# The second MLP matrix in seven products on six input tiles instead of four

## The chip, the cores and the metric

The kernel runs on one core of one Trainium2 chip. The metric is the device time of one execution in microseconds (us). Before the change it is 2111.66 us, the median of three runs (2111.22 to 2114.75).

## The reference, cut to what matters

A two-layer encoder trunk on 256 rows of 2048 columns, in float32: attention, an MLP, again attention, again an MLP. The change touches the two MLPs, `h + (relu(norm(h) @ w1)**2) @ w2`:

```python
def sq_relu_mlp(h, g, w1, w2):
    a = jax.nn.relu(rms_norm(h, g) @ w1)   # w1: 2048 x 8192
    return (a * a) @ w2                    # w2: 8192 x 2048
```

## The kernel before, in words

**Products.** Every matrix product is float32 made of three: the stationary activations and the moving weights are each split into a rounded part `hi` and a rest `lo`, and `three` (lines 403 to 407) adds hi x hi, hi x lo and lo x hi. The activations stay in SBUF as split tiles; the weights stream from memory in *units* of 128 x 1024 (two depth tiles of 128, 512 output columns each). For each unit SP issues a load (`load`, L173), ScalarE rounds it (`issue`, L185: `hi`), VectorE subtracts (L186: `lo`), and TensorE does twelve products of 128 x 512 (two depth tiles, two blocks of 128 rows, three each). The pools hold three `hi` and three `lo` tiles and four raw ones. `fetch` (L189) keeps two units split ahead of the one in use, and three more loaded.

**MLP.** The 8192 hidden columns go in four chunks of 2048 (`NCH`). A chunk has four *pairs*: two pairs of w1 (together 2048 hidden columns), and two of w2, the first and the second pair, which add to the result. A pair is two panels, `a` and `b`, of 512 output columns over a depth of 2048, that is 16 depth tiles: eight units per panel. The first four depth tiles of both panels, eight blocks of (row block, depth half, panel), are done in Strassen-Winograd form: seven products instead of eight, `f0` to `f6` (class `Form`; their weights are called 11, T3, T2, T1, 21, T4, 22). Each is a tile of 128 x 1024 and six TensorE products (`form_products`, L419). The remaining units are `a2` to `a7` and `b2` to `b7`.

**Weight sums.** VectorE forms T1 = 12 - 11, T3 = 22 - 12, T2 = T3 + 11 and T4 = 21 - T2 (`make`, L729, L742). T2 overwrites 12, T4 overwrites 11, T1 and T3 have rooms of their own under the tag "bias" (two buffers; for the first pair of an MLP in the attention's large buffer). `bring` (L724) loads the four tiles for the next pair and `prepare` (L744) places loads and sums by the number of direct units left before the next pair begins. `sums` (L231) forms the four activation sums for the fast form, split into `Sh` for hidden tiles.

**Correcting adds.** ScalarE copies two product sums out of PSUM (L835, L838: `p7`), VectorE adds them back (L819 after f2, L827 after a2). The accumulator that these adds read is written next by f3 and by the first b unit.

**Order.** `plan_mlp` (L132) writes the order of a pair out by hand: f0, b5 of the pair before, f1, b6, f2, b7, f3, then its head. For a first w2 pair ("late") this is a2 f4 a3 f5 b2 f6 b3 a4 a5 b4 a6 a7, for the second ("") a2 f4 a3 f5 a4 f6 a5 a6 a7 b2 b3 b4. b5 to b7 go into the next pair. `keep_order` (L35) fixes the written order on VectorE, ScalarE, TensorE and SP, so an instruction waits behind all that is written before it on its engine.

**Evacuation.** When a panel is done, a w2 pair adds it to the residual (`residual`, L510). A w1 panel is transposed (L279) into `z`, sent through memory (`carry`: row store L289, column loads L295), then squared and split in steps (`take`, L756: relu, rounded square, square on ScalarE; `low`, L768, on VectorE). Such steps hang on a list, `fill`, of which one entry is written after each direct unit; the numbers in `uses` (L791) say in which. Panels 0 and 1 of a chunk come from its first w1 pair, 2 and 3 from its second. Depth tiles 0 to 3 of w2 are panel 0's, 4 to 7 panel 1's, and so on, so a6 of a w2 pair reads panel 3's.

Of the kernel before, what the change touches and what calls it, by code (L numbers as in the profile page):

```python
# [20 lines left out]
H = 16  # L21
# [10 lines left out]
REL = 384  # L32

# [13 lines left out]
def trunk(ctx: ExitStack, tc: tile.TileContext, xT, xr, gs, hg, bf, wgate, w_in, w_oa, w1a, w2a,  # L47
          w_kv, w_qb, w_ob, w1b, w2b, rel, out):
# [35 lines left out]
    ones = const.tile([P, T], F32, name="ones")  # L84
    V.memset(ones, 1.0)
    warm = ps_o.tile([P, 512], F32, name="pt", tag="po")
    for _ in range(11):
        TE.matmul(warm[:, :P], ones[:, :P], ones[:, :P], start=True, stop=True)
# [18 lines left out]
    class Form:  # L107

        def __init__(self, pair, i):
            self.pair, self.name = pair, ("11", "T3", "T2", "T1", "21", "T4", "22")[i]  # L110
# [8 lines left out]
    class Pair:  # L119
# [3 lines left out]
        def __init__(self, src, first, order, third):  # L123
            self.src = [[src[first + q * 8 + u] for u in range(8)] for q in range(2)]
            self.third, self.ps, self.t, self.room, self.units = third, None, {}, None, (9, 8, 7, 6, 5, 2)
            self.head = {"early": "a2 f4 a3 f5 b2 f6 b3 a4 b4 a5 a6 a7", "late": "a2 f4 a3 f5 b2 f6 b3 a4 a5 b4 a6 a7",
                         "": "a2 f4 a3 f5 a4 f6 a5 a6 a7 b2 b3 b4"}[order]

        def items(self, names):
            return [(self, "abf".index(i[0]), int(i[1])) for i in names.split()]  # L130

    def plan_mlp(w1, w2, tail):  # L132
        n, pairs = w1.shape[0] // NCH, []
        for c in range(NCH):
            for src, late in ((w1, ""), (w2, "late")):
                for q in range(2):
                    pairs.append(Pair(src, c * n + 16 * q, (late if pairs else "early") if q == 0 else "", len(pairs) % 2 == 0))
        pairs[0].units, pairs[1].units, pairs[2].units = (15, 13, 11, 8, 10, 8), (9, 8, 7, 6, 3, 2), (9, 8, 7, 6, 1, 2)
        plan, rest = [], [(tail, 0, u) for u in range(KT // UA - 3, KT // UA)]
        for p in pairs:  # L140
            f = p.items("f0 f1 f2 f3")
            plan += [f[0], rest[0], f[1], rest[1], f[2], rest[2], f[3]] + p.items(p.head)
            rest = p.items("b5 b6 b7")
        plan += rest
        units.extend(Form(p, i) if q == 2 else p.src[q][i] for p, q, i in plan)
        return plan
# [6 lines left out]
    plan_a = plan_mlp(w1a, w2a, tail_a)  # L153
# [5 lines left out]
    plan_b = plan_mlp(w1b, w2b, tail_b)  # L159
# [16 lines left out]
    def issue(parts=1):  # L176
# [3 lines left out]
        if not cuts:  # L180
            raw, cuts = raw.pair.t[raw.name], [slice(0, UN)]
        hi = wsp.tile([P, UN], F32R, name="hi")
        lo = wsp.tile([P, UN], F32R, name="lo")
# [3 lines left out]
        ready.append((hi, lo))  # L187

    def fetch(ahead=AHEAD, early=EARLY):  # L189
        while (units or raws) and len(ready) <= ahead:  # L190
            issue()
        while units and sum(1 for r in raws if r[1]) < early:
            load()
        return ready.popleft()
# [36 lines left out]
    def sums(a, fs):  # L231

        w = [wk.tile([P, 512], F32, name="sum", tag="wk") for _ in range(2)]

        def part(i):
            v = w[i // 2][:, i % 2 * 256 : i % 2 * 256 + 256].rearrange("p (g t) -> p g t", g=2)
# [6 lines left out]
        hi, lo = ([fs[k][:, i * 512 : (i + 1) * 512] for i in range(2)] for k in range(2))  # L243
        for i in range(2):
            S.activation(hi[i], w[i], AF.Copy)
        yield
        for i in range(2):
            V.tensor_tensor(lo[i], w[i], hi[i].bitcast(F32), op=ALU.subtract)
        yield

    def split_turned(t, n, which, into, fs=None):
        x = acts.tile([P, 2, GH, T], F32R, name="act")
        y = qkv.tile([P, GH, REL], F32, name="bias")[:, :, :T]
# [45 lines left out]
    def turned(name="q"):  # L299
        z = qkv.tile([P, GH * T], F32, name="z")  # L300
        return z, qkv.tile([P, GH * T], F32, name=name, tag=name, bufs=2)
# [52 lines left out]
    class RowStats:  # L354
# [27 lines left out]
        def spread(self):  # L382
            self.R = const.tile([P, T], F32, name="R")
            pr = ps_o.tile([P, 512], F32, name="pt", tag="po")
            rb = wk.tile([P, NB, P], F32, name="rb", tag="wk")
            for b in range(NB):
                V.tensor_scalar(rb[:, b], ones[:, :P], self.r[:, b : b + 1], None, op0=ALU.mult)
# [31 lines left out]
    def form_products(ps, hi, lo, x, fs, i):  # L419
        for g in range(2):  # L420
            if i in (0, 4, 5):
                xh, xl = (x[2 * g + (i > 0)][:, k, (i == 5) * P : (i == 5) * P + P] for k in range(2))
            else:
                c = {3: 0, 2: 1, 1: 2, 6: 3}[i] * 256 + g * P
                xh, xl = (fs[k][:, c : c + P] for k in range(2))
            three(ps[i not in (4, 5)][i in (1, 5)], xh, xl, hi, lo, g, i < 2 and g == 0, i < 2 and g == 1, skip_group_check=True)
# [204 lines left out]
    wgr = const.tile([P, KT * H], F32, name="wgr")  # L631
    ct = {}

    def gates(x, st):
# [5 lines left out]
        def clear():  # L640
            G.memset(w.bitcast(F32), 0.0)

# [11 lines left out]
        c = const.tile([H, T], F32, name="gc")  # L654

        def logs():
# [14 lines left out]
            V.tensor_tensor_scan(c, ones[:H, :], z, 0.0, op0=ALU.mult, op1=ALU.add)  # L671
# [8 lines left out]
        def turn_c():  # L680
            pc = ps_o.tile([P, 512], F32, name="pt", tag="po")
            ct["cq"] = const.tile([P, NB, H], F32, name="cq")
            for b in range(NB):
# [5 lines left out]
                [step], [step], [step], [step], [], [turn_c]]  # L689

    def decay_bias(g, box):
        nb = qkv.tile([P, GH, REL], F32, name="bias")
# [12 lines left out]
    for g in range(NG):  # L705
# [12 lines left out]
        zk, k = turned("k")  # L718
        v = qkv.tile([P, NB, 512], F32, name="v")
# [4 lines left out]
    def bring(p, name):  # L724
        t = qkv.tile([P, UN], F32, name="w" + name, tag="kv"[name[1] == "2"], bufs=2)
        SY.dma_start(t, p.src[int(name[1]) - 1][int(name[0]) - 1])
# [229 lines left out]
```

## Time and profile before

| what | value |
|---|---|
| median of three runs | 2111.66 us |
| profiled execution, its own time | 2112.75 us |
| span of that execution, first to last instruction | 2111.0 us |
| VectorE busy | 1590.9 us, 75% |
| ScalarE busy | 1194.8 us, 57% |
| memory read, written | 450.01 MB, 39.87 MB |

The profile is taken from one execution. A line such as `L186 DVE TENSOR_TENSOR lo<-raw,hi 128x1024 ... x642` is a group: line of the kernel, engine, operation, output from inputs, shape, count; then busy time in us and the mean of one in ns, then the engine's idle time just before them with what ended it. PE is TensorE, PEld its weight loads, DVE VectorE, ACT ScalarE, POOL GpSimd, SP the engine that issues DMAs. Rows in order of time begin with the start in us from the span's start and the duration. In the waits, "A <- B: total, times, longest" says that A's engine stood idle until B was done.

### The profile page before, as it was taken

The page shows a single profiled execution, that of the slowest core. Times are in us where ns is not written, and L with a number is a line of the kernel's source. Part 1 is how long each engine was busy: PE and PEld are TensorE (multiplying, and loading weights), DVE is VectorE, ACT ScalarE, POOL GpSimd, SP SyncE. Part 2 cuts the span into 40 slices and gives each one's busy share as a digit, 9 for nine tenths or more (in the row PEclk, how much of TensorE's full clock was granted, in tenths as well). Part 3 has the DMA queues.
Part 4 walks back from the last instruction along what each step waited for, and adds up shares of the span by engine and source line. Part 5 has one row for each costly group of instructions (what it writes and reads, how often), then busy time and mean ns, then how long its engine had stood idle before and what let it go on. Part 6 is the DMA issues. An engine that isn't in the chain of part 4 may idle for free.

```text
span 2111.0 us, 25847 instructions
## 1 busy us (share of the span) xinstructions
PE 2101.8 (100%) x9326; PEld 1739.0 (82%) x9326; DVE 1590.9 (75%) x1811; ACT 1194.8 (57%) x1431; POOL 48.7 (2%) x47
## 2 busy tenths in 40 slices
PE   9999999999999999999999999999999999999999
PEld 7788888888888888888888888888888888888887
DVE  6777666887788777778767577778877877887775
ACT  6544455665466566556575445456654654665653
POOL 1011000000000000000001000000000000000000
PEclk9999999999999999999999999999999999999999
DMA  8787778776676677577678777777766766766774
GB/s 282 227 263 232 237 246 276 236 239 229 216 238 214 210 249 239 181 239 267 192 239 265 236 234 233 229 269 247 251 220 215 232 226 214 246 211 209 243 239 146
DMA packets 183888, 491.61 MB, mean 233 GB/s; under 512 B 36928, under 2 KB 73936, under 8 KB 183760
## 3 DMA queue, kind: packets, MB, share of 16 engines
q1 hardware_dynamic: 183760, 489.96, 71.1%
q8 instruction: 73, 1.20, 0.2%
q14 instruction: 55, 0.45, 0.1%
HBM read 450.01 MB, written 39.87 MB: 232 GB/s over the span
## 4 chain that ended last, share of the span: by engine, by line
PE 96%; DMA 1%; DVE 1%; SPq 0%; ACT 0%; issue 0%; DVEq 0%; ACTq 0%
PE acc L406 25%; PE acc L407 25%; PE acc L405 25%; PE s L405 6%; PE s L406 6%; PE s L407 6%; DMA raw<-in_w_in 1%; PE po L563 1%; PE s L532 1%; DVE lo L186 1%; DMA raw<-in_w_ob 0%; PE po L564 0%; PE s L531 0%; ACT hi L185 0%; PE s L652 0%
## 5 line engine op out<-in xcount | busy, mean ns | idle before, releaser
L186 DVE TENSOR_TENSOR lo<-raw,hi 128x1024 fp32r<-128x1024 f32 (+1 forms) x642 | 780.4, 1217 | 303.5 <-ACT hi L185 282.1
L185 ACT ACTIVATE hi<-raw 128x1024 fp32r<-128x1024 f32 (+1 forms) x642 | 678.0, 1057 | 500.8 <-PE acc L407 393.6
L405 PE MATMUL acc<-hi,act 128*128 128x512 f32 x2304 | 905.9, 393 | 0.4 <-ACT hi L185 0.4
L406 PE MATMUL acc<-lo,act 128*128 128x512 f32 x2304 | 897.6, 390 | 3.4 <-DVE lo L186 3.4
L407 PE MATMUL acc<-hi,act 128*128 128x512 f32 x2304 | 897.0, 389 | 0.0
L406 PEld LDWEIGHTS acc<-lo,act 128*128 128x128 f32 x2304 | 432.7, 188 | 95.9 <-DVE lo L186 6.5
L405 PEld LDWEIGHTS acc<-hi,act 128*128 128x128 f32 x2304 | 432.7, 188 | 90.3 <-ACT hi L185 1.5
L407 PEld LDWEIGHTS acc<-hi,act 128*128 128x128 f32 x2304 | 432.5, 188 | 90.2 <-DVE act L228 0.3
L185 ACT ACTIVATE hi<-w 128x1024 fp32r<-128x1024 f32 x160 | 169.8, 1061 | 206.5 <-PE acc L407 111.5
L186 DVE TENSOR_TENSOR lo<-w,hi 128x1024 fp32r<-128x1024 f32 x160 | 195.3, 1221 | 106.9 <-ACT hi L185 106.6
L405 PE MATMUL s<-hi,act 128*128 128x512 f32 x448 | 174.4, 389 | 0.0
L407 PE MATMUL s<-hi,act 128*128 128x512 f32 x448 | 174.3, 389 | 0.0
L406 PE MATMUL s<-lo,act 128*128 128x512 f32 x448 | 174.3, 389 | 0.0
L185 ACT ACTIVATE hi<-wT 128x1024 fp32r<-128x1024 f32 x60 | 63.8, 1063 | 71.5 <-PE acc L407 49.0
L186 DVE TENSOR_TENSOR lo<-wT,hi 128x1024 fp32r<-128x1024 f32 x60 | 73.5, 1225 | 39.0 <-ACT hi L185 39.0
L405 PEld LDWEIGHTS s<-hi,act 128*128 128x128 f32 x448 | 84.1, 188 | 17.5
L407 PEld LDWEIGHTS s<-hi,act 128*128 128x128 f32 x448 | 84.1, 188 | 17.5
L406 PEld LDWEIGHTS s<-lo,act 128*128 128x128 f32 x448 | 84.1, 188 | 17.4
L742 DVE TENSOR_TENSOR wT<-w,w 128x1024 f32<-128x1024 f32 x60 | 73.1, 1218 | 0.0
L474 POOL TENSOR_TENSOR rn<-vv,mhalf 128x4 f32<-128x4 f32 x32 | 43.3, 1366 | 388.9 <-DVE vv L473 388.7
L566 ACT ACTIVATE act<-po 128x256 fp32r<-128x256 f32 x32 | 12.3, 385 | 70.2 <-PE po L564 70.2
L567 DVE TENSOR_TENSOR act<-po,act 128x256 fp32r<-128x256 f32 x32 | 13.6, 424 | 34.4 <-ACT act L566 34.4
(164 smaller groups left out, 1410.5 us busy)
## 6 DMA issues: line engine op xcount, KB each, us to landing
raw<-in_w1a SPq DMA_DIRECT2D x96, 512.0 KB, 4.6
raw<-in_w2a SPq DMA_DIRECT2D x96, 512.0 KB, 4.4
raw<-in_w1b SPq DMA_DIRECT2D x96, 512.0 KB, 4.5
raw<-in_w2b SPq DMA_DIRECT2D x96, 512.0 KB, 4.1
raw<-in_w_in SPq DMA_DIRECT2D x94, 512.0 KB, 4.5
raw<-in_w_kv SPq DMA_DIRECT2D x64, 512.0 KB, 4.3
turn<-z SPq DMA_DIRECT2D x60, 512.0 KB, 4.4
q<-turn SPq DMA_DIRECT2D x168, 128.0 KB, 4.0
```

What stands on the lines that cost most here:

```text
L185: S.activation(hi[:, c], raw[:, c], AF.Copy)
L186: V.tensor_tensor(lo[:, c], raw[:, c], hi[:, c].bitcast(F32), op=ALU.subtract)
L405: TE.matmul(ps, xh, wh, start=first, stop=False, **kw)
L406: TE.matmul(ps, xh, wl, start=False, stop=False, **kw)
L407: TE.matmul(ps, xl, wh, start=False, stop=last, **kw)
L474: G.tensor_tensor(rn, vv, mhalf, op=ALU.pow)
L532: TE.matmul(s[:, P : 3 * P], q[:, a, P:T], k[:, a], start=True, stop=True)
L563: TE.matmul(po[:, :T], v[:, 0, a * P : (a + 1) * P], pT[:, :2], start=True, stop=False)
L566: S.activation(o[i][:, 0], po[:, :T], AF.Copy)
L567: V.tensor_tensor(o[i][:, 1], po[:, :T], o[i][:, 0].bitcast(F32), op=ALU.subtract)
L742: V.tensor_tensor(t[name], t[a], t[b], op=op)
```

## The change

In the w2 pairs the seven-product form spans six depth tiles instead of four. The tiles 11, 12, 21, 22 of these pairs are 128 x 1536 (three depth tiles, `WIDE`), loaded from a new layout of w2 (`_wide`), and are used as a full tile (`f`, six products) and a half-width one (`h`, three products). Half-width tiles have one `hi` and one `lo` buffer. The direct units of these pairs are a3 to a7 and b3 to b7. The order of a w2 pair is new ("wide").

Weight sums are written over weights: T1 over 12, T2 over T3, T4 over 11; only T3 has a room, under the tag "bias", which has one buffer now and also serves the attention biases and the gate's small tensors. T2 of a w2 pair is made after h0's products and the unit behind it. The first panel's second correcting add follows a3.

The hidden sums get a third part for depth tiles 4 and 5, made from panel 1. The steps in `uses` and the loads' and sums' places are new. Panel 3 of the hidden tile is taken at b4 (two steps) and a5 (two steps), ahead of a6.

```diff
@@ class Pair
-            self.head = {"early": "a2 f4 a3 f5 b2 f6 b3 a4 b4 a5 a6 a7", "late": "a2 f4 a3 f5 b2 f6 b3 a4 a5 b4 a6 a7",
-                         "": "a2 f4 a3 f5 a4 f6 a5 a6 a7 b2 b3 b4"}[order]
+        def plan(self, rest):
+            made = [self.items(f"f{i} h{i}" if self.wide else f"f{i}") for i in range(7)]
+            own = {"early": "a2 F a3 F b2 F b3 a4 b4 a5 a6 a7", "": "a2 F a3 F a4 F a5 a6 a7 b2 b3 b4",
+                   "wide": "a3 F b3 F a4 F b4 a5 a6 a7"}[self.order].split()
+            plan = made[0] + rest[:1] + made[1] + rest[1:2] + made[2] + rest[2:] + made[3]
...
@@ plan_mlp
+                when = (7, 5, 6, 4, 3, 2) if q else (9, 7, 8, 6, 5, 1) if c else (9, 7, 8, 6, 3, 2)
+                pairs.append(Pair({k: w2f[4 * at + i] for i, k in enumerate(names)}, src, "wide", len(pairs) % 2 == 0, when))
@@ issue
-        hi = wsp.tile([P, UN], F32R, name="hi")
-        lo = wsp.tile([P, UN], F32R, name="lo")
+        n = cuts[-1].stop
+        hi = wsp.tile([P, n], F32R, name="hi" if n == UN else "hih", bufs=3 if n == UN else 1)
+        lo = wsp.tile([P, n], F32R, name="lo" if n == UN else "loh", bufs=3 if n == UN else 1)
@@ fetch
-        while (units or raws) and len(ready) <= ahead:
+        while (units or raws) and sum(1 for r in ready if not r[2]) <= ahead and not (half_next() and any(r[2] for r in ready)):
             issue()
@@ form_products
-        for g in range(2):
+        for g in (2,) if half else range(2):
@@ make
-        if name in ("T1", "T3"):
...
-        elif name == "T2":
-            t[name] = t["12"]
+        if name == "T3":
+            t[name] = prob.tile([P, 9 * 3 * P], F32, name="wT3", tag="p", bufs=1) if p.order == "early" else room("bias", "wT3")
         else:
-            t[name] = t["11"]
+            t[name] = t[{"T1": "12", "T2": "T3", "T4": "11"}[name]]
@@ prepare
-        for name, at in zip(("12", "11", "22", "21", "T1", "T3"), p.units):
+        for name, at in zip(("12", "22", "21", "11", "T3", "T1"), p.units):
@@ take
+            elif n == 1:
+                yield from sums([[t3[:, 2 * j + b : 2 * j + b + 1] for j in range(2)] for b in range(NB)], Sh[c][2:], 1)
@@ turn_hidden
-                    uses = (4, 5, 6, 6 if late else 7) if n % 2 else (4, 5, 7, 8, 9, 10)[: 6 if n == 0 else 4]
+                    uses = ((4, 5, 7, 8, 9, 10), (4, 5, 6, 7, 8, 9), (4, 5, 6, 7), (4, 4, 5, 5))[n]
@@ mlp
-                if u == 0:
+                if u == 0 and not p.wide:
                     make(p, "T2")
-                if u == 2:
+                if u == 2 and q == 2 + p.wide:
                     V.tensor_tensor(p.ps[0][1], p.ps[1][0], p.t["P7"], op=ALU.add)
...
-                if p.fast and (q, u) == (0, 2):
+                if p.fast and (q, u) == (0, p.own):
                     V.tensor_tensor(p.ps[1][1], p.ps[1][0], p.t["P7"], op=ALU.add)
...
                 if k == 0:
                     S.activation(f.ps[0][0], f.ps[1][0], AF.Copy)
+                    if f.wide:
+                        make(f, "T2")
```

184 lines of the change are left out of this document (105 added, 79 removed).

## The prediction

> **What bounds the kernel now.** I read the page first, then busy time by stretch, then the waits, then the order of time inside one pair of the second matrix.
>
> ```profile
> span 2111.0 us, 25847 instructions
> PE 2101.8 (100%) x9326; PEld 1739.0 (82%) x9326; DVE 1590.9 (75%) x1811; ACT 1194.8 (57%) x1431; POOL 48.7 (2%) x47
> DMA packets 183888, 491.61 MB, mean 233 GB/s; under 512 B 36928, under 2 KB 73936, under 8 KB 183760
> ```
>
> TensorE is busy for the whole span. The profiled execution took 2112.75 us, 1.75 more than its span, and 1.09 more than the median of 2111.66. "Busy" could still hide waits, so next come two pairs of w2 in the second chunk (first pair, then second pair):
>
> ```profile
> 630.50:672.70 42.20, 42.20 (x188) 34.91 (x187) 32.44 (x30) 26.96 (x27) 0.00 (x0) 1.00 0.75 246
> 672.70:714.90 42.20, 42.20 (x188) 34.95 (x187) 32.52 (x31) 21.15 (x21) 0.00 (x0) 1.00 0.60 200
> ```
>
> The columns are length, then PE, PEld, DVE, ACT, POOL busy, granted clock, DMA share, GB/s. TensorE never pauses here, at clock 1.00; VectorE stands at 32.4 of 42.2 us (77%). The waits of TensorE and ScalarE:
>
> ```profile
> ACT hi L185 <- PE acc L407: 557.8, 500, 3.5
> DVE lo L186 <- ACT hi L185: 429.4, 463, 3.2
> PE acc L406 <- DVE lo L186: 3.4, 8, 0.8
> ```
>
> ScalarE waits for TensorE to give back a `hi` buffer, VectorE for ScalarE, TensorE for almost nobody. So products saved are time saved, as long as `hi` and `lo` come in time.
>
> **Part 1, products removed.** One unit of twelve products, in order of time:
>
> ```profile
> 493.15 0.39 PE L405 MATMUL acc<-hi,act 128*128 128x512 f32 x1
> 495.87 0.39 PE L405 MATMUL s<-hi,act 128*128 128x512 f32 x1
> 498.59 0.39 PE L405 MATMUL acc<-hi,act 128*128 128x512 f32 x1
> ```
>
> These are the first products of three neighbouring units: 2.72 us per twelve, 0.2267 each. A w2 pair had 7 x 6 = 42 products in seven-product form for four input tiles and 24 for the next two; now it has 7 x 9 = 63 for all six. That is 3 fewer in each of 16 pairs, 48 in all (9112 tensor instructions against 9160): 48 x 0.2267 = 10.9 us saved. That is the whole gain: the weights' bytes are the same.
>
> **Part 2, what VectorE and ScalarE gain in work.** The rows by shape:
>
> ```profile
> L742 DVE TENSOR_TENSOR wT<-w,w 128x1024 f32<-128x1024 f32 x60 | 73.1, 1218 | 0.0
> L248 DVE TENSOR_TENSOR Sh<-sum,Sh 128x512 fp32r<-128x512 f32 x16 | 10.3, 685 | 0.0
> L239 DVE TENSOR_TENSOR sum<-q 128x256 f32<-128x256 f32 x8 | 3.3, 418 | 0.0
> L245 ACT ACTIVATE Sh<-sum 128x512 fp32r<-128x512 f32 x16 | 10.1, 632 | 17.0 <-DVE sum L240 16.7
> L185 ACT ACTIVATE hi<-w 128x1024 fp32r<-128x1024 f32 x160 | 169.8, 1061 | 206.5 <-PE acc L407 111.5 <-DVE lo L186 49.7 <-PE s L407 22.8
> ```
>
> Records overlap a little. A stretch in which VectorE never idles gives the distance from start to start:
>
> ```profile
> 463.79 1.22 DVE L186 TENSOR_TENSOR lo<-wT,hi 128x1024 fp32r<-128x1024 f32 x1
> 464.92 1.22 DVE L742 TENSOR_TENSOR w<-wT,w 128x1024 f32<-128x1024 f32 x1
> 466.06 1.21 DVE L186 TENSOR_TENSOR lo<-raw,hi 128x1024 fp32r<-128x1024 f32 x1
> ...
> 472.47 0.69 DVE L819 TENSOR_TENSOR acc<-s,p 128x512 f32<-128x512 f32 x1
> 473.07 1.22 DVE L186 TENSOR_TENSOR lo<-raw,hi 128x1024 fp32r<-128x1024 f32 x1
> 474.20 1.31 DVE L279 STREAM_TRANSPOSE z<-acc 128x512 f32<-128x512 f32 x2
> 475.43 1.20 DVE L186 TENSOR_TENSOR lo<-w,hi 128x1024 fp32r<-128x1024 f32 x1
> ```
>
> So a slot of 1024 columns is 1.14 us, of 512 columns 0.60, two transposes 1.24. No row has 1536 columns. The bounds are 1.14 and 2 x 1.14; on the line through 0.60 and 1.14 it is 1.68, and I take that, since both rows are plain subtractions of the same kind. A 128-column sum is 0.28 (418 ns less the 266 ns that 256 columns more cost).
>
> The Trainium skill, page "VectorE: DVE Perf Modes", section "Terms", says that the pipe is flushed after every operation and the next can't issue until it is empty. By that the slots would be the whole records, 1.22; the trace disagrees, with starts 1.13 apart for records of 1.22.
>
> Per w2 pair VectorE gains seven half `lo` (7 x 0.60), loses two full ones (2 x 1.14), gains 0.54 on each of four weight sums, and in the first pair also four small sums and one `lo` for them (1.6): +4.1 in the second pair, +5.7 in the first. That is 38 of 41.5 us, 92%, in the first pair: it fits on average. What decides is the order inside.
>
> **Part 3, the first w2 pair of a chunk, step by step.** I count from f0's start on TensorE, were nothing late. f + h is 9 products, 2.04 us, and with the direct unit behind it 4.76. `hi` buffers are three, the half-width one only one, so ScalarE's rounding for f0 starts when b2 of the pair before ends, at -5.44, plus 0.20 (ACT 493.35 in the fence below against the unit's start at 493.15). In VectorE's written order then come: lo f0 (-4.15 to -3.01), four sums (to -2.0); ScalarE rounds the sums (0.63) and only then h0's half, so h0's lo runs -0.7 to -0.1; lo b5 waits for its hi and ends 1.4; lo of the sums 2.0, T1 (1.68) 3.7, lo f1 4.9, lo h1 5.5, lo b6 6.6. T2 now stands behind lo h1 and lo b6, since it overwrites T3, which h1 still reads: its record ends 8.3. hi f2 needs T2: 9.4. lo f2 starts 9.47 and is ready 10.7. f2's second product wants it at 2 x 4.76 + 0.23 = 9.75: **late by 0.9**. Before, T2 stood ahead of lo b6, and that unit covered hi f2.
>
> From 9.47 VectorE is full: lo f2, h2, b7, T4, f3 lead to the first corrective add, which ends at 15.9. f3's first product overwrites the accumulator that this add reads, and would start at 14.28 + 0.9: late by a further 0.6. Then lo h3, a3, two transposes, f4, h4, b3, the low half of the hidden tile for panel 2, and the second add, which now stands after a3 with only f4 and h4 ahead of b3 (before: f4, a3, f5). It ends at 23.5; b3 overwrites what it reads, and b3's place was 21.08. **Together 2.4 us late**; behind it VectorE catches up.
>
> One more wait is certain by order. The hidden tile for panel 3 is squared and split one unit later than before, right ahead of a6, which reads it. The trace has this very sequence:
>
> ```profile
> 493.35 1.06 ACT L185 ACTIVATE hi<-raw 128x1024 fp32r<-128x1024 f32 x1 [0.71 <-PE acc L407]
> 494.32 1.04 ACT L764 ACTIVATE q<-q 128x1024 f32<-128x1024 f32 x1
> 494.44 1.23 DVE L186 TENSOR_TENSOR lo<-raw,hi 128x1024 fp32r<-128x1024 f32 x1 [0.36 <-ACT hi L185]
> 495.59 1.22 DVE L768 TENSOR_TENSOR act<-q,act 128x1024 fp32r<-128x1024 f32 x1
> ```
>
> The low half is ready 3.66 us after the unit's start at 493.15; before, a whole unit stood between (a6 at 498.59). Now a6 starts 2.72 after it and its third product loads that tile at about 2.95: 0.7 late. Each such pair loses 2.4 + 0.7 = 3.1 us. In the first chunk of each MLP the small sums come after lo b5 and ScalarE's rounding of them holds up hi f1; lo f2 is 0.8 later still: 3.9. Six times 3.1 and twice 3.9 make 26.4.
>
> **The second w2 pair** has no small sums or low halves but two residual adds of 0.66 ahead of lo f1. The same count gives lo f2 at 9.2 (wanted 9.75), the first add at 14.4 (f3 at 14.28), the second at 21.0 (b3 at 21.2): 0.1 each, 0.8 for eight. In the last chunk of layer A two transposes for the next stage fall between lo b7 and T4: 1.2 once.
>
> **Edits costed at nothing.** The attention bias has one buffer: its next load is issued 27 units after the last, the last read is in the 19th, so 8 units x 2.72 = 21.8 us cover a landing of 6.5 (row below); were that cover gone, 6.5 a group. The gate's tiles moved into that room are freed one unit earlier by the moved transpose. The 768 KB loads stand on SP's queue where the 512 KB ones did; the row of that size lands in 6.5 us. In a second pair the load of f0's tile stands behind a raw load that waits for lo a5, so it goes out 2.5 us after a4's end, 5.0 ahead of f0's rounding (a4's end to a5's is 7.5); it lands 1.5 late, and T3 (1.68), ahead of lo f0 on VectorE, covers 1.2 of that:
>
> ```profile
> w<-in_w2a SPq DMA_DIRECT2D x32, 512.0 KB, 5.6
> bias<-cd SPq DMA_DIRECT2D x4, 768.0 KB, 6.5
> ```
>
> **The sum.** -10.9 + 26.4 + 0.8 + 1.2 = +17.5 us: 2130.2 against the profiled execution's own 2112.75, and against the median 2129.
>
> **The rivals.**
>
> *VectorE keeps up, and the kernel gets faster.* Place: from b2's end to f2. The chain there is 14.8 us long (lo f0's start to lo f2's end) in the 13.9 that TensorE gives it; shorter by 0.9 it costs nothing, and if the run from f2 to b3 is shorter by 2.4 too, only the wait at a6 stays: 8 x 0.7 = 5.6, so 2106; without it 2101. For it: in the first w2 pair VectorE ran without a break from before 463.79 to 475.43 and TensorE lost nothing. Against it: the chain is 14 VectorE instructions with two waits for ScalarE, and would have to be 6% shorter than their rows. Chance 0.17, at 2101 to 2107.
>
> *Half the lag.* The slots are a few hundredths shorter, or ScalarE reaches h0 earlier: 14 us lost for 10.9 gained, 2107 to 2116. Chance 0.08.
>
> *The second pairs lag too.* They have 0.5 us to spare at f2 and none at f3. If the 768 KB tiles land in 1.5 times 5.6 = 8.4 us, f0's rounding is 3.4 late, 2.2 beyond T3's cover and 1.7 beyond what f2 has to spare: 8 x 1.7 = 14 more, 2143. Against it: the one row of 768 KB shows 6.5. Chance 0.12.
>
> *Whole records.* If VectorE's slots were 0.08 longer, the 28 instructions of the chain would cost 2.2 us more in each of eight pairs: 2147. The overlapping rows speak against it; chance 0.03. (By the Trainium skill's flush, "VectorE: DVE Perf Modes", "Terms", this is what would come.)
>
> That the change saves no products is excluded by the count of instructions.
>
> **How the numbers follow.** The forecast, 2117 to 2140 (first pairs losing 1.8 to 4.5 us each), has 0.60. A measurement of this kernel can tell about 0.2% from no change, 4.2 us: faster is below 2107.4, slower above 2115.9. Faster 0.17, same 0.08, slower 0.75. The range 2104 to 2142 leaves out about half of the first rival, half of the third and the fourth: 0.07 + 0.06 + 0.03.
>
> **What would show it.** Waits of TensorE for VectorE in the w2 stages: at the fast product with `lo` (f2), at f3 and b3 for the corrective adds, and at a6 for the hidden tile's low half; some 26 us in all, in the first pairs of the chunks, at most 1 us each. First pairs take 44.5 us, second pairs 41.6 against 42.17, w1 pairs as before. It is wrong if first pairs take 41.5 to 42.2 (VectorE keeps up), if second pairs take over 43, or if the waits are for loads.

## The result, and the profile after

The changed kernel takes 2150.35 us (median of four runs, 2147.38 to 2150.47) against 2112.32 for the kernel before on the same chip (2111.22 to 2114.75): a ratio of 1.0175, 95% interval 1.0157 to 1.0193, 38 us slower. The forecast was 2129.0, its range ended at 2142. The profiled execution took 2150.24 us. From its page, the span and the engines' busy time:

```profile
span 2148.5 us, 25852 instructions
PE 2110.7 (98%) x9278; PEld 1725.0 (80%) x9278; DVE 1658.4 (77%) x1931; ACT 1217.5 (57%) x1519; POOL 49.1 (2%) x48
```

48 TensorE instructions fewer (9326 before), 120 on VectorE more, and TensorE now has pauses. The six largest waits of TensorE (total, times, longest):

```profile
PE s L438 <- DVE lo L210: 8.4, 14, 0.8
PE acc L438 <- DVE lo L210: 6.1, 16, 0.8
PE acc L437 <- DVE acc L845: 4.0, 8, 1.6
PE s L437 <- DVE s L853: 3.7, 8, 0.5
PE s L437 <- DVE acc L845: 3.2, 8, 0.4
PE acc L439 <- DVE act L796: 3.0, 8, 0.4
```

Before, TensorE waited 3.4 us for `lo` in the whole span. Now it waits 14.5 us for `lo`, and for both corrective adds (L845, L853) and the hidden tile's low half (L796) as well. The two w2 pairs of the second chunk, from f1 to the next pair's f1 (length; PE, PEld, DVE, ACT, POOL busy; clock; DMA share; GB/s):

```profile
642.78:688.28 45.50, 43.33 (x184) 33.80 (x183) 37.42 (x38) 27.47 (x33) 0.00 (x0) 1.00 0.62 211
688.28:730.59 42.31, 41.41 (x182) 33.63 (x181) 34.63 (x35) 21.40 (x24) 0.00 (x0) 1.00 0.52 176
```

Without waits the first would be 42.16 - 0.68 = 41.5 long, and the second, whose h0 lies outside, 40.8. In order of time, TensorE's products that started late, four of the first pair (f2, f3, b3, a6) and three of the second (b5, f2, f3); in brackets the idle time and what ended it:

```profile
648.97 0.50 PE L438 MATMUL s<-lo,Sh 128*128 128x512 f32 x1 [0.77 <-DVE lo L210]
...
654.21 0.47 PE L437 MATMUL s<-hi,Sh 128*128 128x512 f32 x1 [0.41 <-DVE acc L845]
...
661.75 0.47 PE L437 MATMUL s<-hi,act 128*128 128x512 f32 x1 [0.45 <-DVE s L853]
...
677.82 0.50 PE L439 MATMUL acc<-hi,act 128*128 128x512 f32 x1 [0.37 <-DVE act L796]
...
685.64 0.49 PE L438 MATMUL s<-lo,act 128*128 128x512 f32 x1 [0.17 <-DVE lo L210]
...
693.94 0.50 PE L438 MATMUL acc<-lo,Sh 128*128 128x512 f32 x1 [0.50 <-DVE lo L210]
...
699.18 0.47 PE L437 MATMUL acc<-hi,Sh 128*128 128x512 f32 x1 [0.40 <-DVE acc L845]
```

The first four are the waits that the prediction named. The last three were to be 0.1 together. By the prediction's own signs it was wrong if second pairs took over 43 us, or if waits were for loads: from f0 to the next f0 those of chunks 2, 3 and 4 of layer A took 43.6, 43.7 and 44.7. To compare whole pairs I use one measure throughout, the **lateness**: in the rows of TensorE in order of time, what a product's start lies behind the start before it beyond 0.2267 us each, summed from one pair's f0 to the next pair's.

| lateness, us | forecast | measured |
|---|---|---|
| first w2 pairs, chunks 2 to 4 of both MLPs | 6 x 3.1 = 18.6 | 21.8 (five of 3.4, one of 4.6) |
| first w2 pairs, chunk 1 | 2 x 3.9 = 7.8 | 11.4 (5.7 each) |
| second w2 pairs | 0.8 + 1.2 = 2.0 | 12.0 |
| w1 pairs | 0 | 1.4 (1.25 of it in one pair) |
| sum | 28.4 | 46.6 |

46.6 less the 10.9 saved is 35.7. The spans differ by 37.5; the other 2 us lie before the first MLP, whose first fast product with sums starts at 383.67 here and at 381.61 before. Up to there all changed versions have the same instructions, and in 18 further profiles that start came between 379.84 and 384.88: these 2 us are scatter.

### The profile page after: what moved, and what is told of

Read it like the earlier page. It is cut to its first block, busy times and chain, and to the rows that moved or that the text cites. A ratio compares the mean times of both kernels' runs of the same rounds, so it can differ in the third digit from the quotient of the medians.

```text
span 2148.5 us, 25852 instructions
## 1 busy us (share of the span) xinstructions
PE 2110.7 (98%) x9278; PEld 1725.0 (80%) x9278; DVE 1658.4 (77%) x1931; ACT 1217.5 (57%) x1519; POOL 49.1 (2%) x48
## 4 chain that ended last, share of the span: by engine, by line
PE 72%; DVE 14%; DMA 7%; ACT 3%; issue 3%; SPq 1%; ACTq 0%; DVEq 0%
PE acc L439 20%; PE acc L437 20%; PE acc L438 20%; DVE lo L210 7%; PE s L437 4%; PE s L439 4%; PE s L438 4%; ACT hi L209 2%; DVE w L772 2%; DMA w<-in_w2fa 2%; DVE loh L210 1%; DVE wT L772 1%; DMA turn<-z 1%; DMA w<-in_w2fb 1%; DVE z L311 1%
## 5 line engine op out<-in xcount | busy, mean ns | idle before, releaser
L210 DVE TENSOR_TENSOR lo<-raw,hi 128x1024 fp32r<-128x1024 f32 (+1 forms) x610 | 741.0, 1216 | 299.3 <-ACT hi L209 286.2
L209 ACT ACTIVATE hi<-raw 128x1024 fp32r<-128x1024 f32 (+1 forms) x610 | 641.9, 1053 | 411.5 <-PE acc L439 321.0
L437 PE MATMUL acc<-hi,act 128*128 128x512 f32 x2208 | 868.7, 393 | 0.9 <-ACT hi L209 0.6
L439 PE MATMUL acc<-hi,act 128*128 128x512 f32 x2208 | 860.8, 390 | 4.0 <-DVE act L796 3.0
L438 PE MATMUL acc<-lo,act 128*128 128x512 f32 x2208 | 860.8, 390 | 3.9 <-DVE lo L210 3.8
L439 PEld LDWEIGHTS acc<-hi,act 128*128 128x128 f32 x2208 | 414.4, 188 | 94.5 <-DVE act L796 6.4
L438 PEld LDWEIGHTS acc<-lo,act 128*128 128x128 f32 x2208 | 414.6, 188 | 94.3 <-DVE lo L210 8.7
L437 PEld LDWEIGHTS acc<-hi,act 128*128 128x128 f32 x2208 | 414.6, 188 | 87.0 <-ACT hi L209 1.4
L437 PE MATMUL s<-hi,act 128*128 128x512 f32 x416 | 162.7, 391 | 3.7 <-DVE s L853 3.7
L438 PE MATMUL s<-lo,act 128*128 128x512 f32 x416 | 162.3, 390 | 0.5 <-DVE lo L210 0.5
L439 PE MATMUL s<-hi,act 128*128 128x512 f32 x416 | 162.0, 389 | 0.0
L210 DVE TENSOR_TENSOR lo<-wT,hi 128x1024 fp32r<-128x1024 f32 x64 | 78.3, 1223 | 30.9 <-ACT hi L209 30.8
L209 ACT ACTIVATE hih<-w 128x512 fp32r<-128x512 f32 x80 | 50.2, 627 | 63.4 <-PE acc L439 50.1
L210 DVE TENSOR_TENSOR loh<-w,hih 128x512 fp32r<-128x512 f32 x80 | 54.9, 687 | 15.5 <-ACT hih L209 15.5
```

The costliest lines, as they stand in the source:

```text
L209: S.activation(hi[:, c], raw[:, c], AF.Copy)
L210: V.tensor_tensor(lo[:, c], raw[:, c], hi[:, c].bitcast(F32), op=ALU.subtract)
L437: TE.matmul(ps, xh, wh, start=first, stop=False, **kw)
L438: TE.matmul(ps, xh, wl, start=False, stop=False, **kw)
L439: TE.matmul(ps, xl, wh, start=False, stop=last, **kw)
```

## The experiments

All 18 change the changed kernel. The times are medians, beside the lateness of all first and all second w2 pairs.

| run | what differs from the changed kernel | us | first | second |
|---|---|---|---|---|
| (before) | | 2112.3 | 0.1 | 0.0 |
| (changed) | | 2150.4 | 33.1 | 12.0 |
| e1 | load of tile 11 earlier in second pairs | 2142.3 | 33.7 | 4.8 |
| e2 | panel 3's low half earlier | 2149.3 | 28.0 | 18.3 |
| e3 | panel 2's low half later | 2148.8 | 27.7 | 18.9 |
| e4 | T2 earlier | 2140.6 | 30.8 | 10.0 |
| e5 | e1, e2, e4 | 2129.3 | 23.1 | 5.2 |
| e6 | T1, T3 on GpSimd | 2196.0 | 62.4 | 4.3 |
| e7 | e4, small sums earlier | 2138.5 | 26.7 | 8.9 |
| e8 | e5, small sums earlier | 2128.0 | 20.2 | 5.1 |
| e9 | T1 behind T2 | 2134.5 | 24.5 | 8.0 |
| e10 | e9, e1 | 2132.3 | 23.0 | 6.6 |
| e11 | e10, e2, small sums and T3 earlier | 2127.1 | 14.9 | 6.6 |
| e12 | e10, e2 | 2126.4 | 18.3 | 6.7 |
| e13 | e12, T4 later | 2127.9 | 24.2 | 4.3 |
| e14 | e13, e3 | 2119.5 | 13.5 | 4.2 |
| e15 | e14, chunk 1 as the others | 2120.7 | 14.6 | 4.3 |
| e16 | e14, second add ahead of T4 | 2115.7 | 10.6 | 1.9 |
| e17 | e16, chunk 1's small sums earlier | 2116.8 | 14.8 | 1.9 |
| e18 | e16, chunk 1's first sums earlier | 2113.2 | 7.3 | 1.9 |

e17's 14.8 hold 1.6 us from eight products 0.43 apart at about 466 us, where the granted clock was 0.50.

My theory after the result: the second pairs lose because the 768 KB load of f0's tile comes late; the first because of VectorE's order. The rival: VectorE has too much to do, and order only chooses where it shows.

### The late load (e1)

ScalarE at the start of the second pair of chunk 2, then the landing times of the last three of the pair's four loads (view of tile `w`):

```profile
679.86 1.06 ACT L209 ACTIVATE hi<-w 128x1024 fp32r<-128x1024 f32 x1 [3.54 <-DMA w<-in_w2fa]
```

```profile
L761 SPq DMA_DIRECT2D w<-in_w2fa x3: 328/423/431, 663.3 to 672.3; - x3
...
DMA to landing us min/median/max: 7.5/8.9/9.6
```

The last load, of f0's tile, goes out at 672.3, 4.75 us ahead of the place of f0's rounding (5.0 in the forecast), and lands 7.5 later, not 6.5. VectorE, behind T3, stands still for the rounding:

```profile
677.68 1.75 DVE L772 TENSOR_TENSOR wT<-w,w 128x1536 f32<-128x1536 f32 x1
680.96 1.22 DVE L210 TENSOR_TENSOR lo<-w,hi 128x1024 fp32r<-128x1024 f32 x1 [1.53 <-ACT hi L209]
```

e1 issues the load one unit sooner:

```diff
-                when = (7, 5, 6, 4, 3, 2) if q else (9, 7, 8, 6, 5, 1) if c else (9, 7, 8, 6, 3, 2)
+                when = (7, 5, 6, 5, 3, 2) if q else (9, 7, 8, 6, 5, 1) if c else (9, 7, 8, 6, 3, 2)
```

> One edit: in the second w2 pair of every chunk the 768 KB load of f0's tile (11) is issued right behind the load of 22, one direct unit earlier and so ahead of the raw loads that stood between. Theory (the late load): in the changed kernel this load goes out 5.1 us ahead of f0's nominal rounding and lands 7.5 to 8.9 us after its issue, so f0's hi, T3, lo f0 and all behind them are late, and the eight second pairs lose 1.9 to 2.1 us each instead of the 0.1 predicted. With the load about 6 us earlier the row of ScalarE waiting for that load goes from 3.5 us to under 1, the second pairs lose 0.1 to 0.5, the total falls by 8 to 13 us, to 2137 to 2142. Rival (VectorE has too much to do in the second pairs, whenever the tile comes): the second pairs go on losing about 2 us, the total stays within 2 us of 2150.

2142.25 us (ratio to before 1.0140, 1.0125 to 1.0155). The same two windows of e1:

```profile
639.53:684.46 44.93, 42.97 (x184) 33.96 (x183) 38.37 (x39) 27.67 (x33) 0.00 (x0) 1.00 0.64 218
684.46:725.74 41.28, 41.09 (x182) 33.71 (x181) 33.65 (x34) 21.44 (x24) 0.00 (x0) 1.00 0.53 179
```

The second pair is 1.0 shorter, second pairs' lateness falls from 12.0 to 4.8 with the same instructions on VectorE (the windows cut them differently), and ScalarE's waits for these loads fall from 13.4 us to 0.9 in the first MLP and from 8.5 to 4.2 in the second. The theory holds, at the very end of its interval (2142): 8 us.

### Waits taken away one by one (e2, e3)

The edit of e2, and under it that of e3:

```diff
-                    uses = ((4, 5, 7, 8, 9, 10), (4, 5, 6, 7, 8, 9), (4, 5, 6, 7), (4, 4, 5, 5))[n]
+                    uses = ((4, 5, 7, 8, 9, 10), (4, 5, 6, 7, 8, 9), (4, 5, 6, 7), (4, 4, 4, 4))[n]
```

```diff
-                    uses = ((4, 5, 7, 8, 9, 10), (4, 5, 6, 7, 8, 9), (4, 5, 6, 7), (4, 4, 5, 5))[n]
+                    uses = ((4, 5, 7, 8, 9, 10), (4, 5, 6, 7, 8, 9), (4, 5, 6, 8), (4, 4, 5, 5))[n]
```

> One edit: panel 3 of the hidden tile is taken wholly in the four steps behind b4 instead of two behind b4 and two behind a5. Theory (a6's third product waits for the low half, 0.53 us by its row plus 0.1 behind it, in each of eight first w2 pairs): that wait goes, nothing takes its place because a5 and a6 are direct units with VectorE less loaded, total 4 to 5.5 us lower, 2145 to 2146. Rival (VectorE is so far behind there that the wait only moves, to a5 for the lo of its unit or to f0's tile of the second pair): the wait at a6 goes and another of equal size stands at a5 or at the second pair's first products, total within 1.5 us of 2150, or up to 5 us more since ScalarE's two extra instructions then stand ahead of a5's or a6's hi.

> One edit: the last step of panel 2 of the hidden tile (its low half, 1.2 us on VectorE) is done one direct unit later, behind the second corrective add instead of ahead of it. Theory (b3's first product waits 0.62 us for that add in each of eight first w2 pairs, because VectorE's written order is full between f2 and the add): the wait at b3 falls to nothing or 0.1, total 4 to 5.5 us lower, 2145 to 2146. Rival (the lag only moves: VectorE is behind through a4 and the 1.2 us come back as a wait for a later lo or for that low half at a4 or a5): total within 1.5 us of 2150.

2149.31 (1.0162 to 1.0195) and 2148.83 (1.0159 to 1.0189): the rivals hold. The wait at a6, or at b3, is gone, and first pairs gain 5 us; second pairs lose 6 to 7 more. e2 at the start of a second pair, h0 and b5:

```profile
854.60 0.50 PE L438 MATMUL acc<-loh,act 128*128 128x512 f32 x1 [0.33 <-DVE loh L210]
...
855.73 0.50 PE L438 MATMUL s<-lo,act 128*128 128x512 f32 x1 [0.17 <-DVE lo L210]
```

What the first pair gained, the second pair waits, and it waits behind the late load. In e2 a6's wait of 0.64, which stood between that load's issue and f0, is gone, so f0 comes 0.64 sooner after the same issue; in e3 the load of f0's tile lands 7.8 us after its issue on average, against 6.7 in the changed kernel, and why is open. ScalarE's waits for these loads grow from 21.9 us to 26.3 and 25.4. In e12 below, where the load is early and T1 is moved, e2's edit pays.

### T2, and the small sums (e4, e5, e7, e8)

In e4 T2 is made in `issue`, right behind the split of h1, and no longer behind b6's:

```diff
+        if form is not None and form.half and form.name == "T3":
+            make(form.pair, "T2")
...
```

> One edit: in the w2 pairs the sum T2 is made right behind h1's split instead of behind the lo of b6, the unit after it. The chain T2, hi f2, lo f2 then begins 1.14 us earlier. Theory (f2's second product waits for lo f2 because of this order: 0.95 to 1.0 us in first pairs, 0.67 in second ones): the waits at f2 go in both kinds of pair, lo b6 has room enough (b6 comes 4.8 us after h1's split); f3's wait shrinks or stays at 0.6, so the total falls by 8 to 13 us, to 2137 to 2142. Rival (throughput: VectorE is full from f0 to the second corrective add, so an earlier T2 only lets the same lag stand at f3 or b3): f2's wait is replaced by a longer one at f3, total less than 3 us lower.

2140.55 (1.0118 to 1.0148). The waits at f2 are gone as expected, but "lo b6 has room enough" was wrong:

```profile
644.36 0.50 PE L441 MATMUL acc<-lo,act 128*128 128x512 f32 x1 [1.17 <-DVE lo L211]
```

That is b6 in a first pair. Of the 9.8 us between the medians not all is the edit's: the lateness is 5.6 smaller in e4's profile, and its first MLP starts 2.5 sooner. e5 adds e1 and e2, e7 and e8 the small sums one unit earlier (`uses` of panel 1 from (4, 5, 6, 7, 8, 9) to (4, 5, 6, 7, 7, 8), in chunk 1 from (4, 5, 6, 8, 9, 9)):

> Three edits of the earlier runs together: the load of tile 11 one unit earlier in second pairs, T2 right behind h1's split, panel 3's four steps all at b4. With T2 alone (2140.6) the trace kept 1.3 us at b6 in first pairs, 0.6 at a6, and about 1.1 at b6 in some second pairs. Theory (separate causes: load, order, low half): the second pairs' waits and a6's go and nothing takes their place, since the early load leaves the start of a second pair free for what panel 3's low half pushed there; b6's 1.3 in first pairs stays: 2128 to 2134. Rival (the lag is VectorE's total work and only moves): no better than either edit alone by more than 3 us, 2137 to 2141.

> T2 right behind h1's split, as before, and one more edit: the four small sums for depth tiles 4 and 5 are formed one direct unit earlier (two in the first chunk of an MLP), right behind panel 1's low half, their lo one unit earlier too. In the trace with T2 alone (2140.6) VectorE stands still for 1.2 us in each first pair after f0's lo, because ScalarE rounds the small sums ahead of h0's half, and in the first chunks ScalarE stands still for 5.9 us until the small sums come. Theory (this still-stand, not the amount of work, makes lo b6 late by 1.3): b6's wait falls to 0.1 to 0.4 and the first chunks' waits at h0, f0 and f1 (0.8, 0.3, 0.9) go: 8 x 1.0 + 2 x 2 = 12 us lower, 2126 to 2132. Rival (VectorE's work from the first chunk unit on fills it anyway): b6's wait stays over 1, the total within 3 us of 2140.6.

> All four edits that the traces speak for: early load of tile 11 in second pairs, T2 right behind h1's split, panel 3's steps all at b4, small sums a unit earlier. Theory (each wait has a cause of its own in the order or a load): what stays is about 0.7 us per first pair, 0.3 per second pair and some 4 us at the ends of the stages, 13 lost for 10.9 saved: 2110 to 2120. Rival (VectorE's 92 per cent in first pairs is itself the bound, order only chooses where the wait shows): first pairs go on losing 2 or more, 2124 to 2132.

e5 2129.31 (1.0066 to 1.0096): separate causes, as the theory had it. The three edits bring 21 us together and 19 if what each brought alone is added, so e2's, worth 1 alone, seems to count for more beside e1's; e1 and e4 without it were not run. e7 2138.51 (1.0101 to 1.0134): the rival; b6 waits on. e8 2127.98 (1.0056 to 1.0086), in the rival's interval. At this point "VectorE is full" looked right.

### VectorE's work taken away (e6)

```diff
-        V.tensor_tensor(d, a, b, op=op)
+        (G if p.wide and name in ("T1", "T3") else V).tensor_tensor(d, a, b, op=op)
```

> One edit: of each w2 pair's four weight sums, T1 and T3 are made by GpSimd, which is idle in both MLPs, instead of VectorE. VectorE loses 2 x 1.68 = 3.4 us of work in each of 16 pairs; T3 has 14 us and T1 11 us between the place where it is made and its first use, so GpSimd may take three times as long. Theory (VectorE's work ahead of f2 and f3 is what makes TensorE wait, and GpSimd works beside it): the waits at f2, f3 and b3 go, some 2.2 us in first pairs and 1.2 in second ones, total 2118 to 2128. Rival (the two engines read SBUF in each other's way): VectorE's subtractions get longer or start later while GpSimd adds, and the total comes out above 2145, or above 2160 if VectorE stands still for the whole of a GpSimd sum. The Trainium skill, page 'SBUF - State Buffer', section 'SBUF: two separate sides', states an exclusive lock between the two for a VectorE operation with two SBUF inputs, which is the rival's stronger form; no row of this case shows it yet.

2196.01 (1.0360 to 1.0458): the rival's stronger form, with 29.2 us of lateness in w1 pairs too, where T3 is made. GpSimd's two sums for one second pair, then VectorE in the same stretch:

```profile
681.29 3.50 POOL L772 TENSOR_TENSOR wT<-w,w 128x1536 f32<-128x1536 f32 x1 [40.35 <-ACT act L790]
685.68 3.48 POOL L772 TENSOR_TENSOR w<-w,w 128x1536 f32<-128x1536 f32 x1 [0.88 <-DMA w<-in_w2fa]
```

```profile
682.68 3.20 DVE L210 TENSOR_TENSOR lo<-raw,hi 128x1024 fp32r<-128x1024 f32 x1 [2.17 <-ACT hi L209]
685.80 4.44 DVE L796 TENSOR_TENSOR act<-q,act 128x1024 fp32r<-128x1024 f32 x1
```

VectorE's subtractions, elsewhere 1.22, take 3.20 and 4.44: each ends 1.1 us after GpSimd's sum does (684.79, 689.16), so about its whole work lies behind it. The Trainium skill, page "SBUF — State Buffer", section "SBUF: two separate sides", states this exclusive lock; these rows agree. So this run says nothing on VectorE's load.

### The order again: T1 behind T2 (e9 to e12)

In the changed kernel VectorE, in order of time, from T1 to f2's `lo`:

```profile
640.18 1.75 DVE L772 TENSOR_TENSOR w<-w,w 128x1536 f32<-128x1536 f32 x1
641.85 1.22 DVE L210 TENSOR_TENSOR lo<-wT,hi 128x1024 fp32r<-128x1024 f32 x1
...
644.73 1.75 DVE L772 TENSOR_TENSOR wT<-wT,w 128x1536 f32<-128x1536 f32 x1
647.69 1.23 DVE L210 TENSOR_TENSOR lo<-wT,hi 128x1024 fp32r<-128x1024 f32 x1 [1.21 <-ACT hi L209]
```

VectorE is not full: behind T2 it stands still for 1.21 while ScalarE rounds f2, and T1, which only f3 needs, stood ahead. e9 moves T1 into the hole:

```diff
+            if raw.pair.wide and raw.name == "T2" and not half:
+                make(raw.pair, "T1")
...
```

> One edit of the changed kernel: in the w2 pairs the sum T1 (1.67 us on VectorE) is made behind T2, right ahead of lo f2, instead of ahead of lo f1 (h0's lo in the first chunks). In the trace of the changed kernel VectorE stands still for 1.21 us between T2 and lo f2, because ScalarE rounds f2 only when T2 is done; T1 is first read by f3. Theory (order: T1 stands ahead of a chain that is late, though a hole for it is 4 us further on): T2 starts 1.67 earlier, T1 fills the hole, lo f2 is ready about 1.2 us earlier, so f2's wait (0.95 in first pairs, 0.67 in second ones) goes and the 1.2 us that VectorE no longer stands still also shrink the waits at f3 and b3 (0.6 each): 10 to 25 us lower, 2125 to 2140. Rival (VectorE's work is the bound and the hole is not on the path): T1 only delays lo f2 by what it spared before, total within 3 us of 2150.

> T1 behind T2 as in the run before, and the load of tile 11 one unit earlier in second pairs. Theory (two causes): the load alone gave 8 us (2142.3 against 2150.4); beside T1's place it gives 4 to 8 us more, since part of what a late tile cost in second pairs was in the same waits at f2 and f3: 2118 to 2134, and second pairs keep at most 0.3 us of waits each. Rival (T1's place gives VectorE enough slack to hide the late load): no more than 2 us below the run with T1 alone.

> T1 behind T2, early load of tile 11 in second pairs, panel 3's steps all at b4, small sums one unit earlier (two in first chunks), and in the first chunks T3 two units earlier; T2 stays where the change put it. Theory (every wait of the changed kernel comes from the order of VectorE's work or from that load, and with them gone the 48 products saved are time saved): what stays is some 0.3 us per first pair and 2 to 3 us at the stage ends: 2112.6 - 10.9 + 2.4 + 2.5, 2103 to 2110, faster than the kernel before by 0.1 to 0.45 per cent. Rival (in the first pairs VectorE's work does not fit, whatever its order): 1 us or more per first pair stays somewhere, 2112 to 2122.

> The run before without the earlier small sums and without the earlier T3 of the first chunks: T1 behind T2, early load of tile 11, panel 3's steps at b4. Theory: the small sums hold up ScalarE and VectorE for 1.2 us in each first pair and cost the first chunks 2 to 3 us of waits at h0, f0 and f1, so this version is 4 to 8 us slower than the run before, 2108 to 2117. Rival (with T1 out of the way that still-stand is hidden, as it was in the run with the small sums moved alone, which gained only 2 us): within 2 us of the run before.

e9 2134.46 (1.0093 to 1.0120): 16 us, the most of any single edit, within the theory's range. In order of time:

```profile
642.44 1.75 DVE L774 TENSOR_TENSOR wT<-wT,w 128x1536 f32<-128x1536 f32 x1
644.11 1.75 DVE L774 TENSOR_TENSOR w<-w,w 128x1536 f32<-128x1536 f32 x1
645.77 1.22 DVE L212 TENSOR_TENSOR lo<-wT,hi 128x1024 fp32r<-128x1024 f32 x1
```

The hole is closed: from T2's start to f2's `lo` it is 3.33 us instead of 2.96, but T1's 1.67 no longer stand ahead, so that `lo` comes 1.3 sooner. e10 2132.31 (1.0084 to 1.0112): between the two answers; with the hole closed, the early load brings 2 us instead of 8. e11 2127.12 (1.0060 to 1.0085) is above even its rival's interval, and e12 2126.43 (1.0053 to 1.0084) is the rival: the small sums' place takes 3.4 us of lateness off the first pairs, but e11's earlier T3 makes the w1 pairs ahead of chunk 1 wait (3.1 us in two pairs), so the two together are worth nothing. e12 differs from e10 by e2's edit alone, and here it brings 6 us: first pairs 23.0 to 18.3, second pairs 6.6 to 6.7, so nothing moved.

### The corrective adds, and chunk 1 (e13 to e18)

In e12 the waits left in chunk 2 are f3's (0.6) and b3's (0.7), both for corrective adds. e13 makes T4 after h3's products, and not after b6's, so that the first add no longer stands behind it:

```diff
+                if u == 3 and q == 3:
+                    make(p, "T4")
...
```

> The last version (T1 behind T2, early load of tile 11, panel 3's steps at b4: 2126.4) with one more edit: T4 of the w2 pairs is made after h3's products instead of after f2's, so that the first corrective add no longer stands behind it on VectorE. In the trace of the last version f3 waits 0.6 us for that add in every w2 pair and b3 0.7 for the second add in first pairs. Theory (order): f3's waits go in both kinds of pair, b3's stays since T4 is still ahead of the second add: 16 x 0.6 = 10 us lower, 2115 to 2119. Rival (VectorE's work is the bound in first pairs): there the 0.6 joins the wait at b3 or shows at f5, and only the second pairs' 8 x 0.6 = 5 are gained: 2120 to 2123.

> The run before with panel 2's low half behind the second corrective add as well (the edit that moved a wait of 0.6 to other places when it was made alone). Theory (order): b3's wait goes too, 8 x 0.7 = 5.6 us lower than the run before, 2109 to 2114. Rival (work): the 1.14 us come back at a4 or f6, as they came back when this edit was made alone; within 2 us of the run before.

> The run before, and the first chunk of each MLP gets the places of the others for its small sums and T3 (one direct unit and two earlier). Theory (every wait of the changed kernel came from the order of VectorE's work or from the one late load, and the 48 products saved are time saved when they are gone): the first chunks' waits at f1 and f2 (0.8 and 1.4 us) go, 3 to 4 us lower than the run before, 2104 to 2110: below the kernel before by 0.1 to 0.4 per cent. Rival (in first pairs the work does not fit): 2111 or more.

e13 2127.87 (1.0059 to 1.0086), beyond even the rival. b3's first product, and VectorE's second add:

```profile
655.71 0.47 PE L439 MATMUL s<-hi,act 128*128 128x512 f32 x1 [1.75 <-ACT hi L211]
```

```profile
654.87 0.69 DVE L858 TENSOR_TENSOR s<-s,p 128x512 f32<-128x512 f32 x1
```

The row names ScalarE's `hi`, but that was done at 650.8; what ended the wait is the add, at 655.56. T4 still stands ahead of this add; where it stood, VectorE now idles 0.5 us for f3's `hi`, so the add ends 18.1 us after f1 instead of 17.5, and TensorE, no longer held at f3, is there 0.6 sooner. With e3's edit as well, e14: 2119.46 (1.0019 to 1.0041); its theory's 5.6 us came out as 8.4, but from e13's 2127.9, so its 2109 to 2114 was missed. e15 gives chunk 1 the others' places, (4, 5, 6, 7, 8, 9) for panel 1 and T3 at 5: 2120.74 (1.0024 to 1.0051), the rival: its waits only moved, 1.8 us of them to the w1 pairs ahead of chunk 1. What the second add reads is ready when h3 ends, so e16 makes it there, and not after a3 (against e14):

```diff
                 if u == 3 and q == 3:
+                    V.tensor_tensor(p.ps[1][1], p.ps[1][0], p.t["P7"], op=ALU.add)
                     make(p, "T4")
...
```

> The run of T4 and panel 2's low half (2119.5) with one more edit: the second corrective add of the w2 pairs is made right behind h3's products, ahead of T4, instead of after a3's. In that run b3 waits 0.77 us for this add in each first pair and 0.26 in each second pair, because T4, h4's lo and b3's lo stand ahead of it on VectorE, though what it reads is ready 4 us earlier. Theory (order): both waits go and T4, 0.6 later, is still early enough for f5: 8 x (0.85 + 0.34) = 9.5 us lower, 2108 to 2113, about the time of the kernel before; what stays is 2.2 us in each first chunk and some 0.1s. Rival (work): the 0.6 us come back at f5 or b4, 2117 to 2121.

> The run before, and in the first chunk of each MLP panel 1's low half and its small sums one direct unit earlier, with T3 where it was. Theory: f1's and f2's waits there (0.8 and 1.4 us) shrink to about 1.3 in all with b5's: 1 to 3 us lower than the run before, 2106 to 2112. Rival (VectorE is full from the panel's transposes on, so the wait moves to h0 and b5, as in the run with T3 earlier too): within 1 us of the run before or up to 1 us more.

> The run with the second corrective add ahead of T4 (2115.7), and in the first chunk of each MLP the low half and the sums of panel 0 one direct unit earlier, into a stretch where VectorE stands still for 1.5 and 2.6 us. In that run f1 waits 0.8 us and f2 1.4 in each first chunk, since VectorE works without a break from the panel's transposes on and panel 0's last subtractions (1.3 us) stand at the head of that stretch. Theory (order): those 1.3 us, done earlier, take 0.8 off f1 and 1.2 off f2: 2 x 2 = 4 us lower, 2110 to 2113.5, no different from the kernel before by more than 0.1 per cent. Rival (the stretch is fixed by its transposes, which wait for TensorE): no change, 2114.5 to 2117.

e16 2115.71 (1.0008 to 1.0026), between the two: the waits for the add are gone, but b3 is 0.34 late for its own `lo`. e17, with panel 1 in chunk 1 at (4, 5, 6, 7, 8, 9): 2116.78 (1.0015 to 1.0032), closest to the rival. e18, with `uses` of panel 0 in chunk 1 from (4, 4, 5, 6, 7, 8) to (4, 4, 5, 5, 6, 7), 2113.21 against 2112.62 for the kernel before beside it, ratio 1.0003 (0.9994 to 1.0012): in the theory's interval, and no different from the kernel before. In its profile the lateness of the w2 pairs is 9.2, the saving 10.9; that execution, at 2110.48, was the shortest of eleven. No version beats the kernel before.

So VectorE's work does fit: e18 does all of it, on the same engine, and its first pairs lose 0.6 to 1.5 us instead of 3.4 to 5.7.

## Why the prediction was wrong

**Part 1** (10.9 us saved) holds: 48 instructions fewer (the pages count 9326 and 9278; the prediction's 9160 and 9112 stand in no view and are as far apart), and in e16, where it has almost no wait (0.08), the second pair takes 40.90 us from f1 to the next f1, against 42.16 before: with the 0.08 taken off, 1.34 less for six products, 0.22 each.

**Part 2** holds. A sum of 1536 columns was to take a slot of 1.68; T1 at 640.18 and the next `lo` at 641.85 are 1.67 apart, for a record of 1.75. By the flush rule of the Trainium skill, page "VectorE: DVE Perf Modes", section "Terms", the slot would be the record; the trace disagrees here too. VectorE's 38 us of work in a first pair came as 37.4 us busy in the window above.

**Part 3, the first pair step by step,** holds for its four places. Forecast: f2 0.9, f3 0.6, b3 the other 0.9 of 2.4, a6 0.7. Idle in the rows: 0.77, 0.41, 0.45, 0.37; late in fact by 1.06, 0.65, 0.69, 0.64. TensorE's rows are 0.39 long and start 0.2267 apart, so the idle time, counted from the end of the row before, leaves out some 0.16, and the product behind the late one comes 0.08 to 0.11 later again. With some 0.4 in steps of about 0.1 this makes 3.4 against 3.1. The forecast of 3.9 for **chunk 1** was too small by 1.8: there T1 is made two units before the pair and so stood ahead of h0's `lo` as well (e9, which moves T1, took 1.3 off; e18 1.8 with panel 0's sums).

**The step that failed is "The second w2 pair"**: 0.1 for each, 0.8 in all, and 1.2 once; measured 12.0. The 1.2 came, at f3 of layer A's last chunk. The 0.8 was 10.8, of two parts.

The smaller part is f3 itself. In e1, where the load is in time, the first add ends 14.48 after f0, as counted (14.4), but these 0.2 behind f3's place at 14.28 make f3 and the product behind it 0.43 late together: with small steps 3.6 us in the eight pairs instead of 0.8.

The larger part, 7.2, is the late load. In **Edits costed at nothing**, "it lands 1.5 late, and T3 covers 1.2 of that" leaves 0.3, and these were set at nothing. They fit into the 0.5 to spare at f2; but f3 has "none", as the prediction says itself among its rivals, so all that goes past T3 arrives at f3. The eight second pairs of the changed kernel show it, in order of the time from issue to landing of f0's tile. In the second column stands how much later than right behind T3 its `lo` starts:

| landing, us | `lo` of f0 late, us | lateness of the pair, us |
|---|---|---|
| 5.3 | 0 | 0.45 |
| 5.6 | 0 | 0.45 |
| 6.6 | 0.70 | 1.14 |
| 6.6 | 0.72 | 1.19 |
| 6.8 | 0.88 | 1.33 |
| 7.5 | 1.60 | 2.07 |
| 7.5 | 1.59 | 3.21, 1.2 of it for the two transposes |
| 7.6 | 1.77 | 2.22 |

Each pair loses f3's 0.45 and the whole of the second column. The cover of 1.2 was right (1.26 in e1), and 6.5 us for the landing was close to the mean, 6.7; the lead was 4.75 instead of 5.0, and the rounding starts 0.1 behind the landing. So a landing beyond 5.9 us is paid in full, and a landing below it brings nothing back: the mean alone would cost 0.8 a pair. The row that gave 6.5 is a median of four loads, which took 6.1 to 8.1. The medians of the changed kernel's DMA issues (count, size, us to landing) are over all four tiles of a pair; in the second pairs the tile ahead of f0's took 7.6 to 10.6:

```profile
w<-in_w2fa SPq DMA_DIRECT2D x32, 768.0 KB, 7.6
w<-in_w2fb SPq DMA_DIRECT2D x32, 768.0 KB, 7.4
nb<-cd SPq DMA_DIRECT2D x4, 768.0 KB, 6.4
```

What spreads the landings was not tested by itself. Other loads on the same queue are the likely reason: in e1 f0's tile goes out about 3 us behind the pair's tile before it instead of about 7, and lands after 8.5 on average (6.9 to 9.4) instead of 6.7.

This is the mechanism of the rival "The second pairs lag too", which put a landing of 8.4 and 14 us to it at a chance of 0.12; e1 gave 8 us back by the issue time alone. What e1 leaves, 4.8, is the 3.6 at f3 and the forecast 1.2; e16, whose edits beside e1's are of order, leaves 1.9.

The other rivals fell: VectorE did not keep up, the lag was not halved, and the slots are not whole records. That a6's and b3's waits would add up was tacitly taken; e2 and e3 show that, beside a late load, they don't.

## What to carry to other kernels

A share of busy time tells whether work fits, not whether it comes in time: compare each instruction's place in the engine's written order with the first use of what it makes, and look for a hole further on that it could fill. Here such moves and one load took 37 of 38 us back with no work removed. Judge an edit by the sum over the stages and not by the wait it aims at, since a wait that goes often comes back at the next place. Cost a transfer by the spread of its landings and not by one median, and carry what its cover leaves over to every later place, down to the one with nothing to spare.

## What was not expected of the hardware

- VectorE's subtraction of two tiles stands still while GpSimd sums two others: 1.22 us became 3.20 and 4.44 beside sums of 3.50 and 3.48, and the run lost 46 us on the changed kernel though VectorE had 32 sums fewer.
- A wait in TensorE's rows is not the whole loss: 0.77 idle at f2 is 0.95 late from start to start, since rows of 0.39 start 0.2267 apart, and the next product comes a further 0.11 late.
- Loads of one size in one queue land far apart: f0's 768 KB tile in 5.3 to 7.6 us in the eight second pairs of one execution, the attention's four loads of that size in 5.4 to 8.4.
